# Fixing the written order of a stage of first products: four engines pinned, row dots at an even pace, dependent steps issued later

## The chip, the cores and the metric

The kernel runs on one core of a Trainium2 chip. The metric is the device time of one execution in microseconds. TensorE (PE) multiplies matrices, VectorE (DVE), ScalarE (ACT) and GpSimd (POOL) work on tiles in on-chip memory, and SyncE (SP) and POOL issue DMA transfers, which 16 DMA engines carry out.

## What is computed

One layer of a diffusion backbone. A front part (adaLN, input projections, a bidirectional RG-LRU and gated linear attention) gives 512 latent tokens of width 1024. The case is about the channel mixer behind it, which picks for every token and each of 8 heads 16 of 16384 experts:

```python
q = (u @ w_q).reshape(bsz, t, PEER_HEADS, 2, PEER_DQ // 2)
s = jnp.einsum("bthpd,hpkd->bthpk", q, keys)
s1, i1 = lax.top_k(s[..., 0, :], PEER_TOPK)
s2, i2 = lax.top_k(s[..., 1, :], PEER_TOPK)
...   # 256 sums of pairs, the best 16 give expert and softmax weight
act = gelu(einsum("td,tkd->tk", xb, u_tab[eb])) * wb     # first products
y = einsum("tk,tkd->td", act, v_tab[eb])                 # second products
```

u_tab and v_tab hold 16384 rows of 1024 floats each.

## The kernel before

The 512 tokens are four tiles of 128. Tiles t0 and t1 take the experts' rows by gathers: POOL asks with an indirect DMA for one row per token (`gather`, 128 rows of 4 KB), and VectorE forms the dot with the token (`u_row`, L895) or, later, adds the weighted row to the output (`v_row`, L943). Tiles d0 and d1 are computed densely: all 128 blocks of u_tab go through TensorE (`d_scores`, L991), a gelu puts the result into the array A (128 blocks of 256 columns), A is multiplied by a matrix of weights built from one-hot products, and all blocks of v_tab go through TensorE (`d_out`, L1052).

There are three stages after the front part.

First products. Two Python streams are merged by two counters called clock: `pe_list` writes the dense blocks and, between the first 34, the q products (`q_mm`, L732) and score products (`s_mm`, L742) of d0 and d1; `dve_list` writes the selections (`select`, four heads at a time) and, between their steps, dots of t0 and then of t1 as their experts become known. A step's number in a `yield` is what it adds to its stream's clock. The order that the engines get in this stage is chosen by the framework's planner from what is written. Dots use four buffers called ring and, while selections last, two called rz for every third row. When the planner's clock reaches block 121 the dots stop.

One-hot stage (`w_hot`, `w_mm`, `w_mul`, with `v_load_pairs` and `v_pairs`). In the written order for ScalarE, TensorE and VectorE, 32 iterations each build the weights of 8 tokens, multiply them into A (L1024), and take four v rows of t0 through TensorE (L934). Their gathers are asked for one iteration ahead, into ring and ring_s.

Second products. For each of 128 blocks, `v_split` writes a high and a low part of the weights (gh, gl) and of the block (vh on ScalarE, L1038, and vl on VectorE, L1040); every sixth block is used as it is. Then `d_out` multiplies. Between blocks stand the dots of t1 that are left and the 128 v rows of t1 (`rest`), an even share per block. TensorE, ScalarE and VectorE keep the written order here, POOL does not. vl has two slots, under the tag u_d, in which the first products keep the tokens:

```python
vl = B.tile([128, D], F32R, name="vl", tag="u_d", bufs=2)
```

Of the kernel before, what the change touches and what calls it, by code (L numbers as in the profile page):

```python
# [43 lines left out]
A1 = 88  # L44
# [3 lines left out]
def tile_kernel(ctx, tc, x, cx, pos, ada_w, cols, rows, consts, w_in, wgate, w_g, w_out, w_q, keys_t,  # L48
# [585 lines left out]
    za_s, zs_s = ExitStack(), ExitStack()  # L634
# [23 lines left out]
    zs = pool(zs_s, "zs", side="right")  # L658
    sel_i = {t: kb.tile([128, NSEL], I32, name=f"sel_i{t}") for t in GT}
# [4 lines left out]
    kt = zs.tile([128, 16, 128], F32, name="kt")  # L664
# [62 lines left out]
    def q_mm(ts, h):  # L727
        p = bank("pq")
        for j in range(2):
            w = wq.pop(h * 2 + j)  # L730
            for k in range(KD):
                PE.matmul(p[:, j * 256:(j + 1) * 256], w[:, k], pair_u(ts, k), start=(k == 0), stop=(k == KD - 1))  # L732
        q = zs.tile([128, 2, 2, 128], F32, name="q", bufs=2)
        S.copy(q, p.rearrange("p (j t i) -> p j t i", j=2, t=2))
        return ts, h, q
# [17 lines left out]
    def select(t, h0, nh):  # L753
        s = ss_[t, h0 // 4][:, h0 % 4 * 2:]
        if t in DT and t not in d_stage:
            d_stage[t] = (zs.tile([128, NSEL], I32, name="ei", bufs=1),
                          zs.tile([128, 3, NSEL], F32, name="est", bufs=1))
# [8 lines left out]
        for a0 in range(0, 2 * nh, 4):  # L766
            for a in range(a0, a0 + 4):
                v, i, z = at(a, 0)
                V.max(v, z)
            for a in range(a0, a0 + 4):  # L770
                v, i, z = at(a, 0)
                V.max_index(i, v, z)
            yield 2.5
            for a in range(a0, a0 + 4):
                v, i, z = at(a, 0)
                V.match_replace(z, v, z, NEG)
            for a in range(a0, a0 + 4):
# [6 lines left out]
            yield 1.4  # L784
        tf = tmp([128, nh, 2, TOPK], "tf", bufs=1)
# [14 lines left out]
        yield 1.5  # L800
# [22 lines left out]
        c0 = h0 * TOPK  # L823
        if t in GT:
            dst, wv = sel_i[t], sel_w[t][:, c0:c0 + nh * TOPK]
        else:
# [5 lines left out]
        S.activation(sv, sv, AF.Exp)  # L832
# [4 lines left out]
        eq = zs.tile([128, 4, TOPK, TOPK], F32, name="eq")[:, :nh]  # L837
        V.tensor_tensor(eq, ei[:, :, :, None].to_broadcast([128, nh, TOPK, TOPK]),
                        si[:, :, None, :].to_broadcast([128, nh, TOPK, TOPK]), op=OP.is_equal)
        G.tensor_tensor(eq, eq, sv[:, :, None, :].to_broadcast([128, nh, TOPK, TOPK]), op=OP.mult)  # L840
# [8 lines left out]
    def open_l():  # L849
# [10 lines left out]
        L["a"] = [(0, pool(ctx, "a1p").tile([128, A1, 256], F32, name="A1"))]  # L860

    def open_l2():
        zs_s.close()
        L["a"].append((A1, pool(ctx, "a2p").tile([128, 128 - A1, 256], F32, name="A2")))
        L["abp"] = pool(ctx, "abp")

    def a_of(b, n=1):
        lo, tl = L["a"][b >= A1]
        return tl[:, b - lo] if n == 1 else tl[:, b - lo:b - lo + n].rearrange("p b t -> p (b t)")

    def turn(t):
# [6 lines left out]
        p = bank("ptr")  # L878
        for i in range(3):
            PE.transpose(p[:, i * 128:(i + 1) * 128], st[:, i], ident)  # L880
        pv = p[:, :384].rearrange("p (j t) -> p j t", j=3)
        for i in range(3):
            S.copy(L["st"][i][:, j], pv[:, i])
        S.activation(L["st"][3][:, j], pv[:, 2], AF.Copy, scale=-1.0)


# [5 lines left out]
    def u_row(t, k):  # L892
        more = "sel" not in done and k % 3 == 2
        g = gather(peer_u, sel_i[t][:, k:k + 1], zs.tile([128, D], F32, name="rz", bufs=2) if more else ring())
        V.scalar_tensor_tensor(g, g, 1.0, u_n[t], op0=OP.mult, op1=OP.mult, accum_out=act[t][:, k:k + 1])  # L895

    def u_done(t, h):
        a = act[t][:, h * TOPK:(h + 1) * TOPK]
        S.activation(a, a, AF.Gelu)
        V.tensor_mul(a, a, sel_w[t][:, h * TOPK:(h + 1) * TOPK])  # L900

    def turn_i(t):
# [3 lines left out]
        PE.transpose(p[:, 0:128], f, ident)  # L906
        V.tensor_copy(L["ix"], p[:, 0:128])  # L907
# [77 lines left out]
    def d_scores(b):  # L985
        ut = ld.pop(b)
        if b % 2 == 0:
            ld["ps"] = bank("pds2")
        p = ld["ps"][:, b % 2 * 256:b % 2 * 256 + 256]
# [3 lines left out]
        if b % 2:  # L993
            S.activation(a_of(b - 1, 2), ld["ps"], AF.Gelu)  # L994
# [23 lines left out]
    def w_mul(t, n0, p):  # L1018
        pv = p.rearrange("p (n b) -> p b n", n=4)
        for lo, tl in L["a"]:  # L1020
            c = DT.index(t) * 128 + n0
            nb = A1 if lo == 0 else 128 - A1
# [37 lines left out]
    def u_next(t):  # L1060
# [4 lines left out]
        u_row(t, k)  # L1065
        if k % TOPK == TOPK - 1:
            u_done(t, k // TOPK)
            if k == NSEL - 1 and t == t0:
                turn_a(t0)
        return True  # L1070

    def row_u():
        return u_next(t0) or (not left[t0]["u"] and u_next(t1))

    done = set()

    def pe_list():
# [22 lines left out]
        open_l()  # L1100
        seq = [("u", 0), ("u", 1)]
# [5 lines left out]
        last = None  # L1107
        for n, (kind, b) in enumerate(seq):
            if n + 3 < len(seq):
                u_load(*seq[n + 3])  # L1110
            if kind == "w":
                if b % 2:
                    last = q_mm(DT, b // 2)
                    yield 7.
                continue
            if b == A1:
                while "sel" not in done:
                    yield None
                open_l2()
# [8 lines left out]
        done.add("u")  # L1128

    def dve_list():  # L1130
        for t in (t0, t1, d0, d1):
            for h0, nh in (((0, 2), (2, 2), (4, 4)) if t == t0 else ((0, 4), (4, 4))):
                while (t, h0 + nh - 1) not in done:
                    yield 1.35 if row_u() else None
                owed = 0.0
                for c in select(t, h0, nh):
                    yield c
                    owed += c * ROWS
                    while owed > 1.32:
                        owed -= 1.32  # L1140
                        if row_u():
                            yield 1.32
            if t in DT:
# [4 lines left out]
        done.add("sel")  # L1148
        while left[t1]["u"] and "end" not in done:
            yield 1.55 if row_u() else None  # L1150

    ROWS = 0.9
    streams = [pe_list(), dve_list()]
    clock = [0.0, 60.0]
    while streams[0] or streams[1]:
        i = 0 if streams[0] and (clock[0] <= clock[1] or not streams[1]) else 1
# [3 lines left out]
        elif c is None:  # L1160
            clock[i] = clock[1 - i] + 0.5
# [4 lines left out]
    ET = mybir.EngineType  # L1166
    PIN = {ET.Activation, ET.PE, ET.DVE}
    wb = [(t, n0) for t in DT for n0 in range(0, 128, 4)]
    with tc.manual_schedule(engines=PIN):
        gz = v_load_pairs(0, 1)  # L1170
        hot = [w_hot(*wb[n]) for n in range(2)]
        for n in range(0, 64, 2):
# [6 lines left out]
            for q in p:  # L1179
                w_mul(*q)  # L1180
    for b in range(4):
# [111 lines left out]
```

## Time and profile before

| | us |
|---|---|
| median of three runs | 1570.47 |
| lowest and highest | 1569.88, 1573.06 |
| the profiled execution | 1570.65 |
| its span, first to last instruction | 1568.8 |

| engine | busy us | share of the span |
|---|---|---|
| PE | 1468.1 | 94% |
| DVE | 1191.9 | 76% |
| POOL | 653.5 | 42% |
| ACT | 533.2 | 34% |

The execution moved 484.30 MB at a mean of 309 GB/s. The shares are averages over stages with different limits, so they are to be read stage by stage.

### The profile page before, as it was taken

What the parts mean: (1) busy time and instruction counts of PE and PEld (TensorE: products, weight loads), DVE (VectorE), ACT (ScalarE), POOL (GpSimd) and SP (SyncE); (2) the same over time, 40 slices, a digit from 0 to 9 for tenths busy, and PEclk for the clock granted to TensorE, in tenths of its full rate; (3) what the DMA queues carried; (4) which work ended last, traced back from release to release, by engine and by line L of the source; (5) the groups of instructions that cost most, each with busy time, mean ns of one, the idle gap of its engine ahead of it and who ended that gap; (6) DMA issues with size and microseconds to landing.
All of it is one profiled execution on the core that took longest, in us unless ns stands there. A gap on an engine that the chain in (4) does not pass through costs nothing.

```text
span 1568.8 us, 20348 instructions
## 1 busy us (share of the span) xinstructions
PE 1468.1 (94%) x6668; PEld 1099.7 (70%) x6668; DVE 1191.9 (76%) x2942; ACT 533.2 (34%) x1033; POOL 653.5 (42%) x651
## 2 busy tenths in 40 slices
PE   7899999999999959998999999999979899999995
PEld 2678778468888748887888886555556676666663
DVE  5889975427999999986555545666669898988987
ACT  3657874112211211210110004455433333434333
POOL 0111100004556456475444435666535555544540
PEclk9999999999999979999999999999999999999998
DMA  9655531627899979999999998999999999999995
GB/s 372 194 185 178 160 94 54 255 85 284 309 382 331 331 259 360 346 368 351 373 377 361 389 365 279 353 354 349 345 330 367 346 393 384 379 384 363 382 369 208
DMA packets 152570, 484.30 MB, mean 309 GB/s; under 512 B 14864, under 2 KB 36752, under 8 KB 152336
## 3 DMA queue, kind: packets, MB, share of 16 engines
q0 software_dynamic: 79072, 287.87, 50.2%
q1 hardware_dynamic: 73392, 195.13, 33.5%
q8 instruction: 53, 0.87, 0.2%
q14 instruction: 53, 0.43, 0.1%
HBM read 477.69 MB, written 5.24 MB: 308 GB/s over the span
## 4 chain that ended last, share of the span: by engine, by line
PE 38%; DVE 26%; DMA 16%; issue 10%; POOL 4%; ACT 4%; DVEq 0%; POOLq 0%; ACTq 0%; SPq 0%
PE pds L991 14%; DMA ring<-in_dram,sel_i 11%; PE yv L934 7%; DVE ring L895 6%; PE pwb L1015 4%; PE pw L687 4%; POOL ring L888 3%; DVE rz L895 3%; PE ya L1052 2%; DMA rz<-in_dram,sel_i 2%; PE pq L732 1%; DVE y L943 1%; DMA wada<-in_dram 1%; DMA adw<-in_dram 1%; DVE vl L1040 1%
## 5 line engine op out<-in xcount | busy, mean ns | idle before, releaser
L888 POOL DMA_INDIRECT ring<-in_dram,sel_i x334 | 403.3, 1207 | 404.6 <-DVE ring L895 150.1
L991 PE MATMUL pds<-u_d,ut_s 128*128 128x256 f32 x2048 | 450.7, 382 | 5.0 <-DVE ix L907 5.0
L991 PEld LDWEIGHTS pds<-u_d,ut_s 128*128 128x128 f32 x2048 | 391.8, 192 | 59.1 <-DVE ix L907 5.4
L895 DVE SCALAR_TENSOR_TENSOR ring<-ring,u_n 128x1024 f32<-128x1024 f32 x206 | 255.7, 1246 | 102.1 <-DMA ring<-in_dram,sel_i 100.6
L943 DVE SCALAR_TENSOR_TENSOR y<-ring,act,y 128x1024 f32<-128x1024 f32 x127 | 162.6, 1280 | 37.2 <-DMA ring<-in_dram,sel_i 36.3
L1052 PE MATMUL ya<-vl,gh 128*128 128x512 f32 x428 | 139.3, 407 | 24.9 <-DVE vl L1040 24.6
L1052 PE MATMUL ya<-vh,gh 128*128 128x512 f32 x428 | 142.6, 415 | 2.6 <-ACT vh L1038 2.6
L1040 DVE TENSOR_TENSOR vl<-vt_s,vh 128x1024 fp32r<-128x1024 f32 x107 | 132.8, 1241 | 4.1 <-ACT vh L1038 4.1
L1052 PE MATMUL ya<-vh,gl 128*128 128x512 f32 x428 | 133.9, 394 | 0.0
L1038 ACT CAST vh<-vt_s 128x1024 fp32r<-128x1024 f32 x107 | 112.4, 1050 | 51.1 <-DMA vt_s<-in_dram 44.4
L934 PE MATMUL yv<-ring_s,z 128*64 128x512 f32 x256 | 120.5, 602 | 2.6 <-DMA ring_s<-in_dram,ix 2.5
L934 PE MATMUL yv<-ring,z 128*64 128x512 f32 x256 | 117.4, 599 | 0.0
L1052 PEld LDWEIGHTS ya<-vl,gh 128*128 128x128 f32 x428 | 78.3, 190 | 54.9 <-DVE vl L1040 39.4
L994 ACT ACTIVATE A<-pds 128x512 f32<-128x512 f32 x64 | 37.4, 596 | 225.7 <-PE pds L991 214.7
L1037 ACT CAST gh<-A 128x256 fp32r<-128x256 f32 x107 | 43.4, 406 | 191.2 <-PE ya L1052 176.8
L1000 DVE TENSOR_TENSOR ab<-cst,sel_t 128x512 f32<-128x512 f32 x64 | 44.1, 689 | 81.0 <-PE pwb L1015 50.5
L1052 PEld LDWEIGHTS ya<-vh,gh 128*128 128x128 f32 x428 | 80.7, 189 | 30.9 <-issue 9.8
L1052 PEld LDWEIGHTS ya<-vh,gl 128*128 128x128 f32 x428 | 81.0, 189 | 19.7
L888 POOL DMA_INDIRECT ring<-in_dram,ix x64 | 62.7, 980 | 50.8 <-PE yv L934 22.2
L1015 PEld LDWEIGHTS pwb<-ab 128*128 128x128 f32 x512 | 60.2, 191 | 26.4 <-issue 14.8
L1052 PE MATMUL ya<-vt_s,A 128*128 128x512 f32 x168 | 75.5, 592 | 0.0
L888 POOL DMA_INDIRECT ring_s<-in_dram,ix x64 | 61.1, 955 | 33.6 <-issue 13.5
(307 smaller groups left out, 2291.1 us busy)
## 6 DMA issues: line engine op xcount, KB each, us to landing
ut_s<-in_dram SPq DMA_DIRECT2D x144, 512.0 KB
vt_s<-in_dram SPq DMA_DIRECT2D x128, 512.0 KB
adw<-in_dram POOLq DMA_DIRECT2D x34, 512.0 KB
wraw<-in_dram SPq DMA_DIRECT2D x21, 512.0 KB
wada<-in_dram SPq DMA_DIRECT2D x16, 512.0 KB
wq<-in_dram SPq DMA_DIRECT2D x16, 512.0 KB
ring<-in_dram,sel_i POOLq DMA_INDIRECT x334
wo<-in_dram SPq DMA_DIRECT2D x8, 512.0 KB
```

Of the source, the lines that this page charges most:

```text
L687: PE.matmul(p, mix_k(k)[:, t * 128:(t + 1) * 128], wo[k][:, n * 512:(n + 1) * 512], start=(k == 0), stop=(k == KD - 1))
L888: G.indirect_dma_start(out=g, out_offset=None, in_=tab, in_offset=bass.IndirectOffsetOnAxis(ap=ix, axis=0))
L895: V.scalar_tensor_tensor(g, g, 1.0, u_n[t], op0=OP.mult, op1=OP.mult, accum_out=act[t][:, k:k + 1])
L934: PE.matmul(yv[0][h * 64:h * 64 + 64, n, :], z[:, 63 - i:127 - i], g[:, n * 512:(n + 1) * 512], start=(i == 0), stop=(i == 63), skip_group ...
L943: V.scalar_tensor_tensor(L["y"], g, a, L["y"], op0=OP.mult, op1=OP.add)
L991: PE.matmul(p, ut[:, k], u_d[k // 4][:, k % 4].rearrange("p j t -> p (j t)"), start=(k == 0), stop=(k == KD - 1))
L1000: V.tensor_tensor(ab[:, 0], iota[:, None, :].to_broadcast([128, 4, 128]), st[0][:, j, n0:n0 + 4, None].to_broadcast([128, 4, 128]), op=OP. ...
L1015: PE.matmul(p[:, n * 128:(n + 1) * 128], ab[:, 1, n], ab[:, 0, n], start=True, stop=True)
L1037: S.copy(gh, a)
L1038: S.copy(vh, vt)
L1040: V.tensor_sub(vl, vt, vh.bitcast(F32))
L1052: PE.matmul(ya[t][:, n, :], g[:, j * 128:(j + 1) * 128], v[:, n * 512:(n + 1) * 512], start=(b == 0 and i == 0), stop=(b == 127 and i == l ...
```

## The change

The first products after `open_l` become a region in which ScalarE, TensorE, VectorE and POOL keep the written order. The score products of a q product move behind the four dense blocks that follow it, and four blocks share one gelu of 1024 columns out of a PSUM pair. A helper `later(d, fn)` holds back a step until the planner's clock has gone on by d; the exp of a selection, the gelu and the weighting of dots, and the transposes of indices go through it. Dots are written every 2.4 units of the clock in place of a share of each selection step, and the next selection's first half fills the time in which one waits for its exp. POOL's two elementwise steps of a selection go to VectorE. A is allocated in three parts (88, 12 and 28 blocks); the middle part takes the place of the keys and the q buffers. A dot is split into asking (`u_start`) and computing (`u_fin`). Once the first products are over, `u_start` takes its buffer, rw, from the tag u_d. In iterations 2 to 28 of the one-hot stage a dot of t1 is asked for, and computed one iteration later.

```diff
-A1 = 88
+A_PARTS = (0, 88, 100, 128)
...
-        for eng, src, dst in ((V, tv, cs), (G, tf, ce)):
+        for eng, src, dst in ((V, tv, cs), (V, tf, ce)):
...
-        S.activation(sv, sv, AF.Exp)
+        came = []
+        later(8., lambda: (S.activation(sv, sv, AF.Exp), came.append(1)))
...
-        G.tensor_tensor(eq, eq, sv[:, :, None, :].to_broadcast([128, nh, TOPK, TOPK]), op=OP.mult)
+        V.tensor_tensor(eq, eq, sv[:, :, None, :].to_broadcast([128, nh, TOPK, TOPK]), op=OP.mult)
...
+    def later(d, fn):
+        if "l" in done and "u" not in done:
+            pend.append((max(clock) + d, fn))
+        else:
+            fn()
...
-    def u_row(t, k):
-        more = "sel" not in done and k % 3 == 2
-        g = gather(peer_u, sel_i[t][:, k:k + 1], zs.tile([128, D], F32, name="rz", bufs=2) if more else ring())
+    def u_start(t, k):
+        if "u" in done:
+            g = B.tile([128, D], F32, name="rw", tag="u_d", bufs=2)
+        elif "sel" not in done and k % 3 == 2:
+            g = zs.tile([128, D], F32, name="rz", bufs=2)
+        else:
+            g = ring()
+        return t, k, gather(peer_u, sel_i[t][:, k:k + 1], g)
+
+    def u_fin(t, k, g):
         V.scalar_tensor_tensor(g, g, 1.0, u_n[t], op0=OP.mult, op1=OP.mult, accum_out=act[t][:, k:k + 1])
+        if k % TOPK == TOPK - 1:
+            u_done(t, k // TOPK)
...
-        if b % 2 == 0:
-            ld["ps"] = bank("pds2")
+        if b % 4 == 0:
+            ld["ps"] = bank2("pds4")
...
-        if b % 2:
-            S.activation(a_of(b - 1, 2), ld["ps"], AF.Gelu)
+        if b % 4 == 3:
+            S.activation(a_of(b - 3, 4), ld["ps"].rearrange("p h n -> p (h n)"), AF.Gelu)
...
+        region.enter_context(tc.manual_schedule(engines={ET.Activation, ET.PE, ET.DVE, ET.Pool}))
...
                 if b % 2:
+                    if last:
+                        s_mm(*last)
                     last = q_mm(DT, b // 2)
-                    yield 7.
+                    yield 8.1
...
-            if last:
+            if last and b == 34:
                 s_mm(*last)
                 last = None
-                yield 1.1
-            yield 3.5
+            yield 3.45
...
+        if "end" not in done and clock[1] >= due and clock[1] <= clock[0] + 4 and row_u():
+            clock[1] += 1.32
+            due = max(due + PACE, clock[1] - 6)
+            continue
...
+            if 2 <= n:
+                if late:
+                    u_fin(*late.pop())
+                g = n < 30 and u_next(t1)
+                if g:
+                    late.append(g)
...
-                u_next(t1)
+                u_fin(*u_next(t1))
```

## Rows read from the trace of the kernel before

**Rows 1.** The page's chain that ended last: shares by line.

```profile
PE pds L991 14%; DMA ring<-in_dram,sel_i 11%; PE yv L934 7%; DVE ring L895 6%; PE pwb L1015 4%; PE pw L687 4%; POOL ring L888 3%; DVE rz L895 3%; PE ya L1052 2%; DMA rz<-in_dram,sel_i 2%; PE pq L732 1%; DVE y L943 1%; DMA wada<-in_dram 1%; DMA adw<-in_dram 1%; DVE vl L1040 1%
```

**Rows 2.** Busy time of each engine by stage; columns in the first row.

```profile
core 0: us, PE busy (x) PEld busy (x) DVE busy (x) ACT busy (x) POOL busy (x), PEclk, DMA share, GB/s
409.00:950.00 541.00, 513.55 (x2387) 451.37 (x2387) 419.55 (x1510) 75.58 (x150) 282.78 (x277) 0.97 0.94 351
550.00:600.00 50.00, 31.04 (x136) 26.86 (x135) 50.00 (x203) 5.93 (x10) 29.07 (x28) 0.80 0.78 265
750.00:800.00 50.00, 50.00 (x234) 43.98 (x233) 25.99 (x43) 4.92 (x13) 23.19 (x22) 1.00 1.00 379
950.00:1141.00 191.00, 188.20 (x1015) 97.76 (x1014) 121.72 (x342) 92.37 (x306) 117.27 (x121) 1.00 0.94 341
1160.00:1400.00 240.00, 225.61 (x866) 160.57 (x865) 211.55 (x222) 91.72 (x126) 124.79 (x96) 1.00 0.98 372
```

**Rows 3.** TensorE in order of time: start, length, work, [idle before it <-releaser].

```profile
408.92 7.07 PE L991 MATMUL pds<-u_d,ut_s 128*128 128x256 f32 x32
...
537.93 1.71 PE L742 MATMUL pss<-kt,q 128*128 128x128 f32 x8 [3.50 <-ACT q L734]
...
580.43 2.08 PE L742 MATMUL pss<-kt,q 128*128 128x128 f32 x8 [18.96 <-ACT q L734]
582.30 12.43 PE L991 MATMUL pds<-u_d,ut_s 128*128 128x256 f32 x48
...
605.82 110.67 PE L991 MATMUL pds<-u_d,ut_s 128*128 128x256 f32 x512
...
732.27 26.43 PE L991 MATMUL pds<-u_d,ut_s 128*128 128x256 f32 x112 [4.98 <-DVE ix L907]
...
946.35 3.62 PE L991 MATMUL pds<-u_d,ut_s 128*128 128x256 f32 x16
```

**Rows 4.** ScalarE in order of time, at the longest of TensorE's waits.

```profile
578.36 1.28 ACT L832 ACT_TABLE_LOAD   x1 [26.61 <-DVE sw L831]
```

**Rows 5.** One-hot stage: POOL's gathers one iteration apart, and VectorE, in order of time.

```profile
1118.64 0.69 DVE L1000 TENSOR_TENSOR ab<-cst,sel_t 128x512 f32<-128x512 f32 x1 [2.10 <-PE pwb L1015]
...
1119.83 0.94 POOL L888 DMA_INDIRECT ring_s<-in_dram,ix  x1 [0.30 <-issue]
...
1125.84 0.94 POOL L888 DMA_INDIRECT ring_s<-in_dram,ix  x1 [0.30 <-issue]
```

**Rows 6.** Line 895 from 1130 on: durations min/median/max, first and last start.

```profile
L895 DVE SCALAR_TENSOR_TENSOR ring<-ring,u_n x24: 1209/1216/1227, 1400.1 to 1498.7; 128x1024 f32<-128x1024 f32 x24
```

**Rows 7.** VectorE: 409 to 740 whole, line 895 alone; is_equal's group; one product.

```profile
409.00:740.00 331.00, 311.25 (x1326) 0.95 0.92 343
...
409.00:740.00 331.00, 172.87 (x271) 0.95 0.92 343
...
L838 DVE TENSOR_TENSOR eq<-epos,si 128x1024 f32<-128x1024 uint32 x7 | 8.6, 1235 | 0.0
...
491.41 2.93 DVE L900 TENSOR_TENSOR act<-act,sel_w 128x16 f32<-128x16 f32 x1
```

**Rows 8.** Second products in order of time: a gather and its dot, vl, product pairs.

```profile
1401.63 1.68 POOL L888 DMA_INDIRECT ring<-in_dram,sel_i  x1 [1.80 <-DVE ring L895]
...
1402.77 1.22 DVE L1040 TENSOR_TENSOR vl<-vt_s,vh 128x1024 fp32r<-128x1024 f32 x1
...
1404.61 0.61 PE L1052 MATMUL ya<-vh,gl 128*128 128x512 f32 x2
1405.06 0.62 PE L1052 MATMUL ya<-vh,gh 128*128 128x512 f32 x2
...
1410.80 1.23 DVE L895 SCALAR_TENSOR_TENSOR ring<-ring,u_n 128x1024 f32<-128x1024 f32 x1 [1.93 <-DMA ring<-in_dram,sel_i]
```

**Rows 9.** The first gather of a row, and its dot, in order of time.

```profile
371.06 1.02 POOL L888 DMA_INDIRECT ring<-in_dram,sel_i  x1 [3.58 <-ACT s L746]
...
375.33 2.88 DVE L895 SCALAR_TENSOR_TENSOR ring<-ring,u_n 128x1024 f32<-128x1024 f32 x1 [1.12 <-DMA ring<-in_dram,sel_i]
```

More of the change, by code (lines that the diff above doesn't have):

```diff
@@ L823, in select @@
         c0 = h0 * TOPK
+        if t in DT and t not in d_stage:
+            d_stage[t] = (zs.tile([128, NSEL], I32, name="ei", bufs=1),
+                          zs.tile([128, 3, NSEL], F32, name="est", bufs=1))
         if t in GT:
@@ L877, in turn, with rest @@
         V.tensor_copy(st[:, 0:2], e2)
[L878 to L884, printed above, removed]
+        def rest():
+            p = bank("ptr")
+            for i in range(3):
+                PE.transpose(p[:, i * 128:(i + 1) * 128], st[:, i], ident)
+            pv = p[:, :384].rearrange("p (j t) -> p j t", j=3)
+            for i in range(3):
+                S.copy(L["st"][i][:, j], pv[:, i])
+            S.activation(L["st"][3][:, j], pv[:, 2], AF.Copy, scale=-1.0)
+            done.add(("turn", t))
+        later(8., rest)
+    def later(d, fn):
[3 more added lines that the diff above has]
+            fn()
     def gather(tab, ix, g):
@@ L1064, in u_next, with flush @@
         left[t]["u"].pop(0)
[L1065 to L1070, printed above, removed]
+        return u_start(t, k)
     def row_u():
-        return u_next(t0) or (not left[t0]["u"] and u_next(t1))
+        g = u_next(t0) or (not left[t0]["u"] and u_next(t1))
+        if g:
+            u_fin(*g)
+        return g
     done = set()
+    pend = []
+    def flush(all=False):
+        while pend and (all or min(p[0] for p in pend) <= max(clock)):
+            pend.sort(key=lambda p: p[0])
+            pend.pop(0)[1]()
     def pe_list():
@@ L1100, in pe_list @@
         open_l()
+        done.add("l")
         seq = [("u", 0), ("u", 1)]
@@ L1128, in pe_list @@
         done.add("u")
+        flush(True)
+        region.close()
     def dve_list():
[L1131 to L1143, printed above, removed]
+        jobs = [(t, h0, nh) for t in (t0, t1, d0, d1)
+                for h0, nh in (((0, 2), (2, 2), (4, 4)) if t == t0 else ((0, 4), (4, 4)))]
+        nxt = None
+        for n, (t, h0, nh) in enumerate(jobs):
+            while (t, h0 + nh - 1) not in done:
+                yield None
+            cur, nxt = nxt or select(t, h0, nh), None
+            stop = False
+            while t == d1 and h0 == 0 and ("turn", d0) not in done:
+                yield None
+            for c in cur:
+                if c == "second":
+                    continue
+                if c is not None:
+                    yield c * 0.72
+                else:
+                    if not nxt and n + 1 < len(jobs):
+                        t_, h_, n_ = jobs[n + 1]
+                        if (t_, h_ + n_ - 1) in done:
+                            nxt = select(t_, h_, n_)
+                    c = next(nxt) if nxt and not stop else None
+                    if c == "second":
+                        stop, c = True, None
+                    yield c and c * 0.72
+            if h0 + nh == NH and t in DT:
                 if t == d0:
@@ L1147, in dve_list @@
                 yield 1.
[L1148 to L1152, printed above, removed]
+        while "end" not in done:
+            yield None
+    PACE = 2.4
+    due = 70.
+    ET = mybir.EngineType
+    region = ExitStack()
+    clock = [0.0, 52.0]
     streams = [pe_list(), dve_list()]
-    clock = [0.0, 60.0]
     while streams[0] or streams[1]:
+        if "l" in done and "u" not in done:
+            flush()
+        if "end" not in done and clock[1] >= due and clock[1] <= clock[0] + 4 and row_u():
+            clock[1] += 1.32
+            due = max(due + PACE, clock[1] - 6)
+            continue
         i = 0 if streams[0] and (clock[0] <= clock[1] or not streams[1]) else 1
```

73 lines of the change are left out of this document (45 added, 28 removed).

## Prediction

> **What bounds the kernel now.** I read the chain that ended last first: its largest shares are first-product matmuls, the row dots, and landings of gathered rows [rows 1]. No engine leads alone, so I cut the run into stages [rows 2]: the first products (409 to 950), the one-hot stage (950 to 1141), the second products (1141 to 1545) and a tail. The reader should compare the columns of a stage, not the engines' totals. In an undisturbed stretch of the first products TensorE is busy throughout and the DMA engines are too (share 1.00, 379 GB/s); over the whole stage the DMA only moves 351, and one stretch of 50 us has TensorE at 31 and 265 GB/s. So this stage is limited by TensorE wherever nothing goes wrong, and things go wrong in it.
>
> What goes wrong stands in TensorE's order of time [rows 3]: waits of 3.50, 18.96 and 4.98 us, 27.4 in all. The longest is a score matmul waiting for ScalarE's copy of q. ScalarE shows why [rows 4]: it stood 26.61 us in front of an exp whose input VectorE had not written yet, and the copy came behind it. After such a wait TensorE's clock is granted at the lower level for some us, mean 0.80 in that stretch [rows 2], and three blocks take 12.43 us instead of 10.4 [rows 3].
>
> The one-hot stage repeats every 6.0 us with four gathers [rows 5], which is 4 x 0.524 MB / 6.0 us = 349 GB/s; TensorE is busy 188 of 191 us [rows 2], so it is the limit, with the DMA not far behind. The second products have DMA share 0.98 and 372 GB/s from 1160 to 1400 with TensorE at 94% and VectorE at 88% [rows 2]: the DMA is the limit, and the other two follow closely.
>
> **The change part by part.** A gathered row is 128 x 4 KB = 0.524 MB, a dense block as much.
>
> *Order of the first products.* The written order puts four dense blocks between a q product and its score product, issues the exp 8 units of the planner's clock after the subtraction it reads, and likewise the gelu and the transposes of the indices. That removes the waits of [rows 3, 4]. The floor of the stage from its own rows: 512 matmul records in 110.67 us, so 16 a block make 3.45 us and 128 blocks 442; eight q products of 32 such records and score products of 0.9 make 62; together 504 [rows 3]. The stage now takes from 408.92 to 949.97, 541 us. I allow 5 us for what is left: **-32 us**; bounds -37 (floor) and -20 (waits of 12 us in all come back in other places).
>
> *Can DMA and VectorE feed that?* I walked both loops through by the clock values that the code adds. For the old loop this gives 232 dot rows before the one-hot stage and 24 left for the second products, and 24 there are [rows 6]. For the new loop it gives 222 (18 ahead of the first block, 204 beside the blocks), 14 in the one-hot stage and **20 left**. The stage then moves 144 dense loads and 204 rows, 182 MB; in 509 us that is 358 GB/s, under the 379 above. Between 409 and 740, in which the old selections end, VectorE is busy 311.25 us, 172.87 of them with 136 dots, 1.28 each [rows 7]; 138 are left for some 7.3 selections of four heads, 19.0 each. From POOL each gets the weighting of eq and the additions of candidates. VectorE's own is_equal on the shape of the first takes 1235 ns [rows 7]; I take that for each of the two, 21.5 a selection. Until block 100, about 405 us in, that makes 7.3 x 21.5 + 173 rows x 1.28 = 378: it fits with 7% over.
>
> Against that cost stands a gain that I count at nothing: a 16-element VectorE product took 2.93 us in place of some 0.17 while POOL ran its eq product [rows 7]. It would shorten VectorE only, which is not the limit of this stage. POOL's pinned order holds gathers alone, at six buffers (ring and rz), so a row is asked for some 14 us ahead, above the 9.2 us that a gather took under full load [rows 8].
>
> *Array in three parts.* The middle part of 12 blocks opens when the keys and q buffers are done, at block 88, far behind their last use at block 34. One more product per one-hot group, 64 times some 0.3 us, lies in the 2.1 us that VectorE idles in every iteration [rows 5]: 0. Gelu over four blocks is less overhead on ScalarE, idle anyway: 0.
>
> *Fourteen dots in the one-hot stage.* Their buffers (rw) are two slots of the tag u_d, free there; each is read one iteration after it is asked for. An iteration goes from four to five gathers. POOL issues one in 1.24 us [rows 5], 6.2 for five; the DMA needs 2.62 MB / 379 GB/s = 6.9. So 14 x 0.9 = **+12 us**; bounds +3 (POOL's pace) and +19 (every row paid in full at 379 GB/s).
>
> *Twenty dots in the second products.* Now these rows use the four ring slots, with gathers running ahead. In the new code every row asked for once the first products are over takes an rw slot, and that tag's two slots are also those of vl, which VectorE writes for five blocks in six. What is queued behind: VectorE is pinned, so while it waits for a row it can't write the next vl, and TensorE's second product of the block waits for that. Lifetimes [rows 8, 9]: a vl holds its slot for 1.22 us of writing and four of six product pairs at 0.46, 3.3 with handing over, so 2.75 per block. A row holds it from the gather's issue to the end of the dot: 4.27 us to land in a queue with room, and 1.22, so 5.5, at 1.19 rows a block (148 rows over 124 blocks) 6.55. Two slots serve 9.3 us of this in no less than 4.65 us a block, against some 3.1 now (1160 to 1545, 385 us for 125 blocks). The 20 rows stretch over 16.8 blocks: 1.55 x 16.8 = +26 is the lower end. If slots go round in turn, each row's gather starts only when the row before is done: 20 x 5.6 - 16.8 x 3.1 = +60 is the upper end. Blocks without vl and the first rows of both stretches let a gather run ahead, so I take the middle, +43. The four rows fewer take 4 x 0.524 MB / 379 GB/s = 5 off. Together **+38 us**.
>
> The Trainium skill (DMA: Bandwidth & Descriptors, section Anatomy of one DMA) puts a transfer on this path at about 2.0 us plus its bytes at 436 GB/s, an estimated 3.2 us here; the row has 4.27, and the measurement decides. By the Trainium skill's figure the two ends would be +15 and +38.
>
> **Sum.** -32 + 12 + 38 = +18 us on the profiled execution's 1570.65 us (span 1568.8 and 1.85 around it; the median of the three runs is 1570.47): **1588 us**.
>
> **The rivals.**
> 1. *The shared slots cost nothing* (the other side: faster). If the rows' gathers get issued two or more blocks ahead, their landing lies beside the products. For it: POOL is not pinned there and has time. Against it: two slots can't hold two vl and a row in flight, and now four ring slots barely do, with VectorE waiting 1.93 us for one [rows 8]. It decides from a slot sum below 6.2 us a block. Price: -32 + 12 - 5 = -25: 1546 us.
> 2. *A shorter landing.* With gathers one at a time the queue is emptier than at any row shown. The least that rows allow is the issue, 0.94 us, and 0.524 MB at 379 GB/s, 1.38: 2.3 us. Halfway to 4.27, at 3.3, the ends become +16 and +40, the middle +28 less 5, the total near +3: 1573 us. The only unhurried row speaks against it [rows 9]. The Trainium skill's figure above is the rule for such a landing.
> 3. *The change doesn't do what it says.* A fixed order turns every late row into a wait for what is behind it: if VectorE, 93% filled until block 100 (27 us to spare), loses 88 us to landings, the last selection comes 61 us late, and TensorE, which can write eight more blocks (28 us) until two PSUM groups are full, stands 33 us at block 108. Then the first stage gains nothing: +12 + 38 = +50: 1621 us. Against it: in the old trace VectorE was busy 50.00 of the 50 us from 550 to 600 with selections and rows side by side [rows 2].
>
> **How the numbers follow.** Forecast 0.53, rivals 0.27, 0.10, 0.10. The forecast's own range, from the bounds of its terms (not all at one end), is 1570 to 1612. The range for 8 in 10 reaches down to rival 1's value and leaves out its lower half and rival 3: 1546 to 1612. Faster by over 0.2% (3 us, about what a measurement of this kernel can tell): most of rival 1, a little of rival 2 and of the forecast's lower end, 0.31. Same: 0.09. Slower: 0.60.
>
> **What would show it.** TensorE's timeline of the first products without waits over 5 us, from about 409 to 917; ScalarE no longer standing in front of exp for over 10 us. The one-hot stage some 203 us long, its first 14 iterations near 6.9 us. In the second products the dots of the last 20 rows 4.5 to 6 us apart with VectorE idle on landings of rw before most of them, and TensorE idle on vl, clock perhaps falling; blocks before them slightly faster than now. The forecast is wrong if those dots stand some 3 us apart or less, or if TensorE still waits some 20 us in the first products.

## The result and the profile after

| | before | after |
|---|---|---|
| median, lowest to highest (four runs each, same chip), us | 1571.76, 1569.88 to 1574.94 | 1615.27, 1608.13 to 1617.87 |
| profiled execution, its span, us | 1570.65, 1568.8 | 1608.13, 1606.4 |
| PE, DVE, POOL, ACT busy, us | 1468.1, 1191.9, 653.5, 533.2 | 1486.4, 1193.9, 630.4, 527.1 |

The ratio is 1.0267, 95% interval 1.0228 to 1.0307 (below, such intervals stand in square brackets behind the ratio): slower by 2.7%, where 1588 us (1.1% slower) was forecast, with a range up to 1612. The profiled execution of after is the fastest of its four, 7.1 us below the median; in which stage the others are longer no trace shows. Its chain of waits is followed back for some 5% of the span only, so the time is found stage by stage. The borders are the first and last matmul of the first products (pds) and the last of the v pairs (yv); the last column holds the second products and the tail. Every run of this study is in the table, under the name that its experiment has below, beside the ratio of its median to that of the kernel before on its own chip:

| run | chip | front | first products | one-hot | second products | ratio |
|---|---|---|---|---|---|---|
| before | | 408.9 | 541.1 | 191.8 | 427.0 | 1 |
| after | | 402.0 | 508.2 | 209.5 | 486.7 | 1.0267 |
| e0_after | A | 403.8 | 508.2 | 207.3 | 488.1 | 1.0280 |
| e1_ring | B | 404.6 | 508.2 | 190.3 | 422.7 | 0.9770 |
| e1b_ring | C | 402.9 | 508.2 | 210.1 | 419.1 | 0.9814 |
| e2_no_hot_rows | B | 402.9 | 508.2 | 178.8 | 441.7 | 0.9880 |
| e3_own_slot | A | 404.6 | 508.2 | 207.3 | 495.2 | 1.0307 |
| e5_before_shared | B | 412.0 | 542.2 | 178.7 | 511.8 | 1.0542 |
| e6_ahead | B | 403.1 | 508.2 | 192.6 | 482.2 | 1.0144 |
| e7_all_hot | A | 404.2 | 509.0 | 228.1 | 396.9 | 0.9855 |
| e8_no_later | A | 402.6 | 511.0 | 207.4 | 489.3 | 1.0304 |
| e9_no_pin | C | 397.0 | 552.0 | 209.8 | 490.8 | 1.0501 |
| e10_pool_free | C | 404.5 | 509.7 | 209.3 | 490.4 | 1.0298 |
| e14_scores_early | C | 404.7 | 509.4 | 209.6 | 491.1 | 1.0287 |

After against before: -6.9 - 32.9 + 17.7 + 59.7 = +37.6 us of span. The 20 rows left for the second products and the 14 in the one-hot stage are as counted in the prediction.

TensorE's last product of the front, before and after:

```profile
398.34 8.86 PE L732 MATMUL pq<-ut_g,wq 128*128 128x256 f32 x32 [2.31 <-ACT u_d L710]
```

```profile
394.10 7.17 PE L733 MATMUL pq<-ut_g,wq 128*128 128x256 f32 x32 [0.21 <-ACT u_d L711]
```

TensorE of after in order of time, the rows that answer to [rows 3]:

```profile
402.00 4.05 PE L1030 MATMUL pds<-u_d,ut_s 128*128 128x256 f32 x18
...
568.00 17.43 PE L1030 MATMUL pds<-u_d,ut_s 128*128 128x256 f32 x80
585.27 1.05 PE L743 MATMUL pss<-kt,q 128*128 128x128 f32 x8
586.16 103.77 PE L1030 MATMUL pds<-u_d,ut_s 128*128 128x256 f32 x480
...
697.22 114.13 PE L1030 MATMUL pds<-u_d,ut_s 128*128 128x256 f32 x528
```

No row of the stage has a wait in brackets any more. Score products take 1.05 us behind dense blocks, where one waited 18.96 before.

Stages of after (columns as in [rows 2]): the one-hot stage with and without rows of t1, the second products ahead of the late dots, their first stretch, between the stretches, and the second stretch.

```profile
925.00:1030.00 105.00, 98.96 (x477) 47.38 (x474) 74.29 (x216) 42.63 (x144) 73.23 (x71) 1.00 0.96 353
1030.00:1120.00 90.00, 87.53 (x458) 43.94 (x455) 58.69 (x190) 41.47 (x138) 50.62 (x54) 1.00 0.96 350
...
1160.00:1400.00 240.00, 220.43 (x845) 157.49 (x844) 202.12 (x215) 89.62 (x123) 115.27 (x91) 0.99 0.96 366
...
1380.00:1405.00 25.00, 12.93 (x39) 8.06 (x37) 8.66 (x14) 4.90 (x8) 6.35 (x5) 0.80 0.58 214
1405.00:1445.00 40.00, 38.31 (x144) 27.86 (x144) 35.29 (x38) 15.03 (x21) 18.68 (x15) 0.96 0.89 325
1445.00:1545.00 100.00, 60.64 (x179) 41.66 (x178) 44.10 (x64) 19.49 (x29) 19.33 (x19) 0.80 0.54 185
```

Read the last three. In the second stretch TensorE is busy 60.64 of 100 us, VectorE 44.10, the DMA moves 185 GB/s where it moved 372 [rows 2]: nothing is full, so everything waits in turn. The granted clock is 0.80, a mean of its two levels. The 40 us between the stretches run at 325 GB/s; against 372 that is 40 x (1 - 325/372) = 5 us for filling up again, an estimate.

One turn of that stretch, all engines in order of time, which answers to [rows 8]:

```profile
1475.09 1.23 DVE L924 SCALAR_TENSOR_TENSOR rw<-rw,u_n 128x1024 f32<-128x1024 f32 x1 [3.56 <-DMA rw<-in_dram,sel_i]
...
1476.58 1.27 DVE L1078 TENSOR_TENSOR vl<-vt_s,vh 128x1024 fp32r<-128x1024 f32 x1
1476.59 0.94 POOL L910 DMA_INDIRECT rw<-in_dram,sel_i  x1 [5.39 <-DVE rw L924]
1477.90 0.89 PE L1090 MATMUL ya<-vl,gh 128*128 128x512 f32 x2 [1.77 <-DVE vl L1078]
1478.59 1.05 PE L1090 MATMUL ya<-vh,gl 128*128 128x512 f32 x2
...
1481.32 1.23 DVE L924 SCALAR_TENSOR_TENSOR rw<-rw,u_n 128x1024 f32<-128x1024 f32 x1 [3.47 <-DMA rw<-in_dram,sel_i]
```

A dot (1.23 us) frees the slot; POOL, waiting 5.39 us for just that, asks 0.27 us later; 4.73 us after the ask the row has landed and the next dot starts. That is 6.23 us a row. Beside it vl and the products of one block take place, and then all engines stand.

Not every row goes so. 11 of the 20 asks wait for a dot; six wait for TensorE's last product with a vl, whose slot they take. This happens at the second row of each stretch and four times further on, mostly where no vl stands between two rows, and then a gather runs ahead of the dot before it. VectorE and POOL in order of time:

```profile
1455.75 1.23 DVE L924 SCALAR_TENSOR_TENSOR rw<-rw,u_n 128x1024 f32<-128x1024 f32 x1 [7.41 <-DMA rw<-in_dram,sel_i]
1456.99 1.23 DVE L924 SCALAR_TENSOR_TENSOR rw<-rw,u_n 128x1024 f32<-128x1024 f32 x1
...
1486.53 0.94 POOL L910 DMA_INDIRECT rw<-in_dram,sel_i  x1 [2.77 <-PE ya L1090]
1487.61 1.22 DVE L924 SCALAR_TENSOR_TENSOR rw<-rw,u_n 128x1024 f32<-128x1024 f32 x1 [3.53 <-DMA rw<-in_dram,sel_i]
...
1490.92 1.23 DVE L924 SCALAR_TENSOR_TENSOR rw<-rw,u_n 128x1024 f32<-128x1024 f32 x1 [2.08 <-DMA rw<-in_dram,sel_i]
```

The dots at 1487.61 and 1490.92 are 3.31 us apart. Waits of TensorE on vl over the whole run, after and before:

```profile
PE ya L1090 <- DVE vl L1078: 63.0, 30, 10.5
```

```profile
PE ya L1052 <- DVE vl L1040: 24.6, 30, 3.2
```

(total us, times, longest).

### The profile page after: what moved, and what is told of

The parts are those of the page before. It is cut to its first block, busy times and chain, and to the rows that moved or that the text cites. A ratio compares the mean times of both kernels' runs of the same rounds, so it can differ in the third digit from the quotient of the medians.

```text
span 1606.4 us, 20273 instructions
## 1 busy us (share of the span) xinstructions
PE 1486.4 (93%) x6668; PEld 1103.9 (69%) x6668; DVE 1193.9 (74%) x3078; ACT 527.1 (33%) x1001; POOL 630.4 (39%) x579
## 5 line engine op out<-in xcount | busy, mean ns | idle before, releaser
L910 POOL DMA_INDIRECT ring<-in_dram,sel_i x287 | 363.6, 1267 | 374.8 <-DVE y L982 150.1
L1030 PE MATMUL pds<-u_d,ut_s 128*128 128x256 f32 x2048 | 444.8, 379 | 0.0
L924 DVE SCALAR_TENSOR_TENSOR ring<-ring,u_n 128x1024 f32<-128x1024 f32 x159 | 191.8, 1219 | 35.4 <-DMA ring<-in_dram,sel_i 35.3
L1090 PE MATMUL ya<-vl,gh 128*128 128x512 f32 x428 | 146.1, 424 | 63.8 <-DVE vl L1078 63.0
L1090 PE MATMUL ya<-vh,gh 128*128 128x512 f32 x428 | 147.5, 427 | 7.1 <-ACT vh L1076 7.1
L1090 PE MATMUL ya<-vh,gl 128*128 128x512 f32 x428 | 139.7, 409 | 0.0
L1033 ACT ACTIVATE A<-pds 128x1024 f32<-128x1024 f32 x32 | 32.8, 1024 | 302.9 <-PE pds L1030 276.9
L973 PE MATMUL yv<-ring,z 128*64 128x512 f32 x256 | 121.5, 603 | 1.2 <-DMA ring<-in_dram,ix 0.7
L910 POOL DMA_INDIRECT rz<-in_dram,sel_i x63 | 76.6, 1215 | 64.0 <-DVE rz L924 37.2
L924 DVE SCALAR_TENSOR_TENSOR rw<-rw,u_n 128x1024 f32<-128x1024 f32 x34 | 41.6, 1224 | 73.5 <-DMA rw<-in_dram,sel_i 71.5
L910 POOL DMA_INDIRECT ring_s<-in_dram,ix x64 | 63.9, 998 | 44.4 <-DMA ut_s<-in_dram 20.8
```

What stands on the lines that cost most here:

```text
L910: G.indirect_dma_start(out=g, out_offset=None, in_=tab, in_offset=bass.IndirectOffsetOnAxis(ap=ix, axis=0))
L973: PE.matmul(yv[0][h * 64:h * 64 + 64, n, :], z[:, 63 - i:127 - i], g[:, n * 512:(n + 1) * 512], start=(i == 0), stop=(i == 63), skip_group ...
L1030: PE.matmul(p, ut[:, k], u_d[k // 4][:, k % 4].rearrange("p j t -> p (j t)"), start=(k == 0), stop=(k == KD - 1))
L1033: S.activation(a_of(b - 3, 4), ld["ps"].rearrange("p h n -> p (h n)"), AF.Gelu)
L1090: PE.matmul(ya[t][:, n, :], g[:, j * 128:(j + 1) * 128], v[:, n * 512:(n + 1) * 512], start=(b == 0 and i == 0), stop=(b == 127 and i == l ...
```

## The experiments

The theory to test was that late rows in u_d slots go in turn, one landing after another, and cost some 60 us; the rivals, that the loss lies in vl's lost slot, in the order of VectorE, or outside this stage. Chips A, B and C ran the three batches, one each, so a chip can't be told from its batch; every ratio is to the kernel before in the same batch.

**Ring slots instead, in the second products (e1_ring, e1b_ring).**

```diff
-        if "u" in done:
+        if "u" in done and "hot" not in done:
             g = B.tile([128, D], F32, name="rw", tag="u_d", bufs=2)
...
+    done.add("hot")     # behind the one-hot stage
```

> The changed kernel, with one edit: the rows of t1 that are left after the one-hot stage take one of the four ring slots, as in the kernel before, and no longer a slot of u_d that they share with vl; the 14 rows of the one-hot stage keep u_d. Theory 1 (the shared slots cost the second products some 60 us more than before, and rows in the ring cost what the kernel before shows): second products 426.4 - 5 = 421 us, one-hot stage 210 and first products 508 as in the changed kernel, together 402 + 508 + 210 + 421 + 2 = 1543 us (1535 to 1553). Theory 2 (the second products are longer for another reason: the fixed order left their rows to come at a worse place, or the throttled clock of that stretch stays): 1590 us or more. Theory 3 (half of the loss is the slots, as the forecast's middle value had it): about 1570.

Measured: 1525.16 us beside 1559.18 of before, ratio 0.977 [0.9742, 0.9798]. This kernel beats both. The second products took 422.7 us, so the 60 us are gone whole: theory 1. The total is below 1543 because the one-hot stage took 190.3 us on this chip. So the same kernel was run on another one:

> The variant with ring slots in the second products and 14 rows in the one-hot stage once more, for the chip of this batch, beside which the variant with 30 rows in the one-hot stage gave ratio 0.9855 on its own chip. Theory 1 (the one-hot stage moves 350 GB/s on one chip and up to 397 on another, and all else agrees): on a chip with 350, one-hot stage 208 us and ratio 0.984 to 0.988; on one with 397, 191 and 0.977. Theory 2 (the chips differ in the second products too): ratio outside 0.975 to 0.990.

Measured: 1541.90 beside 1571.63, ratio 0.9814 [0.9779, 0.985], one-hot stage 210.1 us, second products 419.1. The absolute time is the 1543 of the first expectation; the ratio is slightly better than theory 1 had it, within its interval. Its stretch with the 20 dots, one row of stages:

```profile
1370.00:1470.00 100.00, 96.41 (x373) 68.94 (x372) 88.58 (x115) 40.37 (x56) 52.99 (x39) 1.00 0.99 376
```

Against 1445 to 1545 of after: 376 GB/s in place of 185, clock 1.00 in place of 0.80. Four slots hide the landings.

**That part alone, in the kernel before (e5_before_shared).**

```diff
-        g = gather(..., zs.tile(..., name="rz", bufs=2) if more else ring())
+        g = gather(..., zs.tile(..., name="rz", bufs=2) if more else
+                   B.tile([128, D], F32, name="rw", tag="u_d", bufs=2) if "w" in done else ring())
```

> The kernel before, with one edit, a part of the change done alone: its 24 rows in the second products take slots of u_d, shared with vl, in place of ring slots. Theory 1 (slots in turn, as the changed kernel shows it: 65 us for 20 rows, 3.25 a row): 1571 + 24 x 3.25 = 1649 us (1635 to 1660). Theory 2 (the loss belongs to the fixed order of the first products or to the split into asking and computing): 1571, unchanged. Theory 3 (the forecast's middle value, 2.15 a row): 1622.

("w" is set behind the one-hot stage.) Measured: 1644.11 beside 1559.18, ratio 1.0542 [1.05, 1.0585], +85 us; its second products are 511.8 - 427.0 = +84.8 us against the trace of before (another chip), 3.5 a row. Theory 1, with 3.25 somewhat low. The order of the first products has no part in it.

**Asked one step ahead (e6_ahead).**

```diff
+            ask = []
             while len(left[t1]["u"]) > NSEL - (h + 1) * TOPK:
-                u_fin(*u_next(t1))
+                if ask:
+                    u_fin(*ask.pop())
+                ask.append(u_next(t1))
                 yield
+            if ask:
+                u_fin(*ask.pop())
```

> The changed kernel, with one edit: in the second products a row of t1 is asked for one step (some 0.8 of a block) before its dot is written, so that a vl stands between asking and computing; the slots of u_d stay shared. Theory 1a (slots in turn: a row's gather can't start before the dot two slots earlier is done, and a row slot is held 6.2 us whatever VectorE does meanwhile): 1600 to 1615 us, as the changed kernel, dots some 6 us apart. Theory 1b (VectorE, standing in front of a landing, holds back vl and by it TensorE): the landings lie beside vl and the products, the loss falls by two thirds, 1565 to 1580 us, dots some 4 us apart.

Measured: 1584.40, ratio 1.0144 [1.0104, 1.0184]; second products 482.2 us, 6 less than the 488.1 of e0_after and 59.5 more than e1_ring on the same chip. In order of time:

```profile
1453.20 1.22 DVE L924 SCALAR_TENSOR_TENSOR rw<-rw,u_n 128x1024 f32<-128x1024 f32 x1
...
1454.70 0.94 POOL L910 DMA_INDIRECT rw<-in_dram,sel_i  x1 [5.80 <-DVE rw L924]
...
1460.15 1.23 DVE L924 SCALAR_TENSOR_TENSOR rw<-rw,u_n 128x1024 f32<-128x1024 f32 x1 [3.37 <-DMA rw<-in_dram,sel_i]
...
1461.65 0.94 POOL L910 DMA_INDIRECT rw<-in_dram,sel_i  x1 [6.01 <-DVE rw L924]
```

The ask is written ahead and still can't be made: POOL waits 5.80 and 6.01 us for the dot that holds the slot, and so do 9 of the 20 asks, for 5.2 to 7.5 us. So theory 1a by the stage: nearly all of the loss is left, though the dots of the long stretch, 5.2 us apart in the mean, come somewhat closer than the 6 it named. The total lies between the two ranges; part of that comes with chip B, where the one-hot stage took 192.6 us, 14.7 less than in e0_after.

**A slot of their own (e3_own_slot).**

```diff
+            L["rwp"] = pool(ctx, "rwp")     # open_a(2)
...
-            g = B.tile([128, D], F32, name="rw", tag="u_d", bufs=2)
+            g = (B.tile([128, D], F32, name="rw", tag="u_d", bufs=2)
+                 if "hot" not in done else L["rwp"].tile([128, D], F32, name="rw", tag="rw", bufs=1))
...
+    done.add("hot")     # behind the one-hot stage
```

> The changed kernel, with one edit: in the second products the rows of t1 have one slot of their own, 4 KB per partition, and vl has both slots of u_d to itself. Theory 1a (the loss is one row in flight at a time: issue, landing and dot one after the other, some 6 us a row, whoever owns the slot): the dots stay some 6 us apart, 1575 to 1600 us. Theory 1b (the loss is that vl must wait for a slot that a row holds): the second products fall to some 430 us, 1535 to 1545 us.

Measured: 1616.34 beside 1568.43, ratio 1.0307 [1.0267, 1.0348], as after or slightly slower. In order of time:

```profile
1475.10 1.23 DVE L926 SCALAR_TENSOR_TENSOR rw<-rw,u_n 128x1024 f32<-128x1024 f32 x1 [3.78 <-DMA rw<-in_dram,sel_i]
...
1476.60 0.94 POOL L911 DMA_INDIRECT rw<-in_dram,sel_i  x1 [5.60 <-DVE rw L926]
1477.91 0.93 PE L1092 MATMUL ya<-vl,gh 128*128 128x512 f32 x2 [1.94 <-DVE vl L1080]
...
1481.41 1.23 DVE L926 SCALAR_TENSOR_TENSOR rw<-rw,u_n 128x1024 f32<-128x1024 f32 x1 [3.55 <-DMA rw<-in_dram,sel_i]
```

The same turn of 6.31 us, with vl's two slots left alone. So it is not vl that lacked a slot: one row in flight at a time is the loss, theory 1a. On the same chip the second products are 495.2 - 488.1 = 7.1 us longer than in e0_after; with a single slot no gather can run ahead any more. My range, 1575 to 1600, was too low.

**The changed kernel again (e0_after).** Unaltered, for the chip.

> The changed kernel once more, unaltered, beside the kernel before on the chip of this batch. In the traces of the other variants the stages before the second products came out shorter than in the first trace of the changed kernel (one-hot stage 191 us against 210, without its rows 179 against 192 in the kernel before), so chips may differ there. Theory 1 (the first pair's chip is slower in the one-hot stage, and the rows cost 12 there elsewhere): one-hot stage 191, first products 508, second products 486, in all about 1590 us, ratio to before about 1.020. Theory 2 (the 210 us come from the shared slots, which the variants lack): one-hot stage 210 here too, 1605 us, ratio 1.027 or more.

Measured: 1608.76 beside 1568.43, ratio 1.028 [1.0231, 1.0329], one-hot stage 207.3 us. By itself that fits theory 2; e1b_ring with 210.1 us, without shared slots in the second products, shows that it goes with the chip: the 14 rows in, A, C and the first pair's have 207 to 210 us, B 190 to 193. The kernel before shows the same: its one-hot stage took 191.8 us in the first trace and 178.7 on B (e5_before_shared, whose edit lies behind it), and its median on B, 1559.18, is 9 to 13 us below those on the others.

**Where rows of t1 stand (e2_no_hot_rows, e7_all_hot).** Both with ring slots in the second products.

```diff
-                g = n < 30 and u_next(t1)
+                g = n < 2 and n > 2 and u_next(t1)     # e2: none
+                g = n < 62 and u_next(t1)              # e7: 30
```

> The changed kernel without rows of t1 in the one-hot stage: all 34 that the first products leave are taken in the second products, in ring slots. Theory 1 (the 14 rows cost the one-hot stage 17.6 us, 1.25 each, and a row in ring slots costs the second products its transfer, 0.524 MB at 372 GB/s = 1.4 us): one-hot stage 192, second products 426 + 10 x 1.4 = 440, in all 402 + 508 + 192 + 440 + 2 = 1544 us, within 6 us of the variant with rows in both. Theory 2 (the one-hot stage is longer for another reason than its rows, as the array in three parts with a third product per group): one-hot stage still 205 or more, 1558 us.

Measured: 1540.07, ratio 0.988 [0.9853, 0.9908]: 15 us above e1_ring in the median. One-hot stage 178.8, second products 441.7. So the 14 rows cost 190.3 - 178.8 = 11.5 us in the one-hot stage of chip B and 441.7 - 422.7 = 19.0 in the second products, 0.82 and 1.36 a row. That is theory 1 in what it says of the stage, not in its 1.25 a row. The two traced executions are only 5.8 us apart, e2's being the fastest of its five and e1_ring's the slowest of its four, so these prices are good to some tenths of a us. The array in three parts costs nothing: e5_before_shared, with two, has 178.7.

> The variant with ring slots in the second products, and rows in 30 iterations of the one-hot stage instead of 14, which leaves 4 for the second products. Theory 1 (a row costs some 0.86 us in the one-hot stage, where TensorE is busy all the time and the DMA has room, and 1.4 in the second products, which the DMA limits): 16 x 0.54 = 9 us less than the variant with 14, ratio to before 0.971. Theory 2 (a row costs its transfer, 1.4 us, wherever it stands): as the variant with 14, ratio 0.977.

Measured: 1544.14 beside 1568.43, ratio 0.9855 [0.9823, 0.9886]. On this chip 16 more rows cost the one-hot stage 228.1 - 207.3 = 20.8 us, 1.30 each; 16 fewer in the second products saved 419.1 - 396.9 = 22.2, 1.39 each (against e1b_ring, on chip C). So theory 2 by the stages; the 0.977 in it was chip B's ratio, and beside e1b_ring's 0.9814 the intervals overlap. On chip B the prices above are nearer to theory 1. Stages within the one-hot stage, one row each of e2_no_hot_rows (B), e1_ring (B) and e1b_ring (C):

```profile
925.00:1030.00 105.00, 105.00 (x598) 55.34 (x596) 74.10 (x241) 57.60 (x185) 70.82 (x76) 1.00 0.99 371
```

```profile
925.00:1030.00 105.00, 103.18 (x529) 50.57 (x526) 83.72 (x246) 52.02 (x167) 79.09 (x79) 1.00 1.02 397
```

```profile
925.00:1030.00 105.00, 97.27 (x468) 47.07 (x465) 74.57 (x216) 43.05 (x144) 73.72 (x70) 1.00 0.95 349
```

The last column tells it: the same gathers move 397 GB/s on B and 349 on C, and TensorE gets through 529 matmul records there and 468 here.

**What gained in the first products (e8, e14, e9, e10).**

```diff
-        if "l" in done and "u" not in done:     # later(), e8 and e14
+        if False:
...
-            if last and b == 34:                # e14 as well
+            if last:
...
-        region.enter_context(tc.manual_schedule(engines={ET.Activation, ET.PE, ET.DVE, ET.Pool}))
+        region.enter_context(tc.manual_schedule(engines={ET.Activation, ET.PE, ET.DVE}))     # e10; e9: no region
```

> The changed kernel, with one edit in the first products: no step is issued later than where it is written (exp right behind the subtraction that it reads, gelu and weighting right behind the last dot, the transposes right behind their inputs); four engines still keep the written order. Theory 1 (the gain of the first products comes in large part from the late steps): TensorE waits again on ScalarE's copies that stand behind exp, first products 520 us or more instead of 508, the total 12 to 30 us longer than the changed kernel. Theory 2 (the gain comes from where the score products are written, four blocks behind their q, and from the even pace; what stands in front of exp no longer reaches TensorE): first products 508 to 512 us, the total as the changed kernel.

> The changed kernel with two parts undone together: no step is issued later than where it is written, and a score product stands one dense block behind its q product, as in the kernel before, not four. Undoing the first alone left the total within 0.3%. Theory 1 (four blocks between q and scores are the cover for ScalarE standing in front of exp): TensorE waits on the copies of q again, some 20 us in all, first products 525 us or more, ratio 1.04. Theory 2 (what ScalarE waits for was VectorE's late subtraction, and the even pace has ended that): no such waits, first products 508 to 512, ratio 1.027 to 1.030.

Measured: ratios 1.0304 [1.0268, 1.034] and 1.0287 [1.0248, 1.0327], first products 511.0 and 509.4 us. The times fit theory 2 both times, but e14_scores_early refutes the reason that the first of them gave: neither the late steps nor the four blocks in front of the scores are what gains. ScalarE does stand in front of exp again in e14_scores_early, but for a few us, and the copies behind it still come in time. Its longest such wait while q products last:

```profile
456.63 0.26 ACT L835 ACTIVATE sw<-sw 128x64 f32<-128x64 f32 x1 [5.27 <-DVE sw L833]
```

> The changed kernel, with one edit: POOL is left out of the engines that keep the written order in the first products. It has gathers alone to order there. Theory 1 (POOL's order costs nothing to leave open, since its gathers have one sensible order): first products 508 us, ratio 1.027. Theory 2 (gathers that are asked for out of turn hold VectorE in front of landings): first products 515 us or more.

Measured: 1617.57 beside 1571.63, ratio 1.0298 [1.0261, 1.0334], first products 509.7 us: theory 1.

> The changed kernel, with one edit: the first products are no region of written order any more, the planner orders ScalarE, TensorE, VectorE and POOL there as before; the late steps, the even pace and the place of the score products stay as written. Theory 1 (the gain of 33 us in the first products comes from the four pinned engines): waits of TensorE on q copies or on index transposes return, first products 525 to 541 us. Theory 2 (it comes from what is written where: score products four blocks behind q, gelu of four blocks): 508 to 513 us, total as the changed kernel, ratio 1.027.

Measured: 1650.01 beside 1571.63, ratio 1.0501 [1.0464, 1.0538], first products 552.0 us. The late steps, the pace and the place of the scores are all there, and the old wait is back. ScalarE, then TensorE, in order of time:

```profile
586.09 0.26 ACT L835 ACTIVATE sw<-sw 128x64 f32<-128x64 f32 x1 [13.26 <-DVE sw L833]
586.25 0.57 ACT L735 COPY q<-pq 128x512 f32<-128x512 f32 x1
```

```profile
396.95 1.03 PE L1030 MATMUL pds<-u_d,ut_s 128*128 128x256 f32 x4
...
400.75 7.13 PE L733 MATMUL pq<-ut_g,wq 128*128 128x256 f32 x32
...
408.61 4.05 PE L1030 MATMUL pds<-u_d,ut_s 128*128 128x256 f32 x18
...
586.87 2.07 PE L743 MATMUL pss<-kt,q 128*128 128x128 f32 x8 [8.76 <-ACT q L735]
588.74 84.18 PE L1030 MATMUL pds<-u_d,ut_s 128*128 128x256 f32 x384
691.28 0.47 PE L950 MATMUL pta<-cst,act 128*128 128x128 f32 x1 [18.36 <-DVE act L936]
```

exp stands in front of the copy of q for 13.26 us, as in [rows 4], and a transpose of the dots' results waits 18.36 us. The 552.0 us hold more than in the other rows of the table: a few matmuls of the first block got ahead of the front's last q product, and the block goes on at 408.61. From there to the stage's end at 948.97 it is 540 us, inside theory 1's range and about what the kernel before took, against 510 in e10_pool_free. So without the written order of ScalarE, TensorE and VectorE the gain of some 31 us is gone, whatever else of the change is there. That this order would do it alone is not shown: the even pace of the dots, the gelu of four blocks and POOL's two steps on VectorE stand in every variant, and none of them was taken back by itself.

## Why the prediction was wrong, point by point

- **First products: right.** -32 forecast, -32.9 measured, no wait of TensorE left. That VectorE and the DMA can feed it held. The reason given was in part wrong: the late steps and the moved scores, which the prediction named as what removes the waits, could both be taken back for 1 to 3 us. The pinned order is what the gain can't do without (e9_no_pin); whether it suffices without the even pace stays open. Rival 3 falls.
- **Front: not in the sum.** -6.9 us, which hides about a quarter of what the two terms below were short by (5.7 and 21.7). Some 4.8 of it stand in the rows above and beside them: the last q product of the front waited 2.31 us for ScalarE's copy of u_d and now 0.21, took 8.86 us and now 7.17, and one of the two score products behind it now stands behind the first block's start. In e9_no_pin, without the region, TensorE waits 2.23 us for u_d again at this place, and the 397.0 there is no shorter front. About 2 us more lie in front of that product; e0_after, the same kernel, lacks them.
- **One-hot stage: mis-sized.** +12 forecast, +17.7 measured, inside its bounds. The step that failed is the rate. I took the 379 GB/s of the first products for five gathers and read the 349 GB/s of [rows 5] as TensorE's pace, since TensorE was busy 188 of 191 us. It was the gathers': with five in an iteration after moved 353 GB/s, with four 350, and an iteration of five took 7.4 us (nine of them from 941.89 to 1008.38, by their asks) where I had 6.9. On chip B the same four gathers an iteration moved 371 to 378 GB/s and the stage took 178.8 us. A TensorE that is busy all the time was no proof that it was the limit. On B the term is +11.5, so the forecast's figure fits that chip alone.
- **Second products: mis-sized, and this decides.** +38 forecast, +59.7 measured, above the term's upper end as well (60 less 5 for the four rows fewer, so +55). The mechanism was right: rows go in turn, VectorE and TensorE stand beside them. The step that failed is the size of the turn, and with it the middle between the ends. The upper end, 20 x 5.6 - 16.8 x 3.1 = 60, took a turn of 5.6 us; the turn shown takes 6.23, since the row lands 4.73 us after the ask in place of 4.27 and the ask stands 0.27 behind the dot. That is 20 x 0.63 = 12.6 us. Taking the middle allowed 17 us for gathers that run ahead. They do run ahead where the prediction said: from the start of the first wait to the end of the last dot the two stretches take 21.9 and 89.8 us, 111.7 in all, against 20 x 6.23 = 124.6. So this was worth 12.9 us, 4.1 less than allowed. The 5 us of filling up behind the first stretch were not in the sum. Together these estimates make the 21.7 us that were short. That the mean, 111.7 / 20 = 5.6 a row, is the upper end's figure is luck, and so is it that the sum with +55, 1606, comes near the profiled 1608.13: the one-hot stage was 5.7 longer and the front 6.9 shorter than in it.
- **The lower end's model** (slots shared in any order, so much lifetime over two) can't hold: in e3_own_slot vl has both slots to itself and the turn is as long, 6.31 us. A row's slot is a chain of its own, gather, landing, dot, gather.
- **Rival 1** (shared slots cost nothing) falls with e5_before_shared. POOL had the time, but most of its asks wait for the slot, 5.39 us in the turn shown.
- **Rival 2** (a shorter landing) falls: 4.73 us from ask to dot in the turn shown, 4.2 to 5.3 in the second stretch behind its first two rows, while the DMA moved 185 GB/s. The row of before that had been taken, 4.27 [rows 9], was too short rather than too long. The estimate of 3.2 us worked out from the Trainium skill (DMA: Bandwidth & Descriptors, section Anatomy of one DMA) is not borne out by the trace: none of these rows landed in under 4.2 us.
- **The bounds.** They were set with not all terms at one end, 1612 at most. Both late terms came out at or above their upper ends together: 1570.65 - 32 + 19 + 55 = 1613, and the median of after is 1615.27.

## What to carry to other kernels

Rows that arrive by gather cost their transfer when several are in flight (some 1.4 us a row here), and issue, landing and use one after the other when one is (6.2): count the slots, not the bytes, before giving a transfer a borrowed buffer. Where a range has an end that is a plain chain of dependences, work its turn out from every step in it, and take off only what a row shows to overlap. A stage that stands at the rate of one resource on one chip may stand at another's on the next, so a price per row there needs both.

## What the runs showed of the hardware that was not expected

- Chips (or the batches that ran on them) differ where gathers alone feed the DMA: 349 GB/s on C and 397 on B with the same five gathers in an iteration; in the second products, which mix gathers and plain loads, they agree (377 GB/s on A, 374 on B, 378 on C, from 1160 to 1380 or 1390 in e0_after, e1_ring and e1b_ring).
- A gather of 128 rows of 4 KB takes 4.2 to 5.3 us from ask to use even when the DMA is half idle (share 0.54); in front of the first dot of each stretch VectorE waited 7.69 and 7.41 us.
- While the engines wait in turn the granted clock falls to a mean of 0.80. From 1472.0 to 1474.5 it is 0.50 (the lower level, 1.2 GHz), and the two-matmul records of the second products take 1.05 us; from 1484 to 1487 it is 1.00 (2.4 GHz), and they take 0.62. In e1b_ring it stays 1.00 over the same dots.
